# First block of a two-block transformer kernel: four pairs of weight parts, an own PSUM bank for the convolution, its layer norm later, both column halves of the projection at once

## The chip, the cores and the metric

One core of a Trainium2 chip runs the whole kernel. The metric is the device time of one execution in microseconds; 1314.99 us is the median of three runs of the kernel before (1314.49 to 1316.63).

## What is computed

Two transformer blocks over 256 tokens of width 1024, in float32. The first block, which the change touches, has three parts, each behind an RMS norm and added to the residual stream:

```python
proj = h @ w_in                      # q, k, v (512 columns each), 8 forget logits, 2 x 512 for the convolution
attn = rmsnorm(forgetting_attention(q, k, v, log_f), attn_out_g)           # 8 heads of 64, causal
conv = silu(layernorm(depthwise_conv31(a * sigmoid(gate)) + b_dw, ln_g, ln_b))
x = x + concatenate([attn, conv], -1) @ w_out
x = x + memory_cross_attention(h, rmsnorm(mem), w_mq, w_mkv, w_mo)         # 256 memory rows, 4 heads of 256
x = x + hierarchical_moe(h, ...)     # 32 experts; a token goes to 2 of the 8 experts of one group
```

The second block (a gated recurrence, a sparse attention and a feed-forward network) is as it was.

## The kernel before

**Matmuls in parts.** A large product is done with both operands split into a rounded part and a remainder. `wload` (line 164) has SP fetch a chunk of 4 x 128 weight rows by 512 columns (1 MB) into one of four `ring` buffers. `wsplit` (170) turns it into two half-chunks; for each, ACT rounds (`wh`, line 184) and DVE takes the remainder (`wl`, line 185) into a pair of the pool `hl`, which has three pairs. TensorE then does three matmuls for each 128 rows: high by high, high by low, low by high. In `dense_T` (216) the tokens are the moving operand (256 columns), so a half-chunk of four 128-column pieces is 24 matmuls of 256 columns; in `dense_nat` (197) the weights are the moving operand, and a half-chunk is 12 matmuls of 512 columns. A ring buffer comes free with its last `wl`, a pair of `hl` with its last matmul.

**The first block (`block1`, 390).** The squares of x are summed on ACT (`sq`), its rows are scaled by DVE and ACT (`ENG[0]`), transposed, and split into `xT`. The products with `w_in` follow: gates and values of the convolution with the forget logits, then q, k, v. The convolution of 31 taps takes two of its four channel groups on DVE, accumulated in the PSUM tile `ca` (452 to 460), and two on ACT and GpSimd: ACT multiplies a shifted slice into a buffer `zt` (three of them), GpSimd adds it to `zc` (466 to 471). Line 462 copies `ca` to `zc`. The attention (527 to 555) has for each pair of heads scores in the PSUM pool `ptr`, exponentials on ACT (324), transposes of the probabilities (540), copies to `PT` and products with the values into two PSUM tiles `po` of one bank each. Both `po` and `ca` are allocated from the pool `pat` of two buffers. After the attention come the keys and values of the memory (`mem_k`, `mem_v`: two chunks of 512 columns each), with the steps of the convolution's layer norm between them (`mu`, `va`, `vr`, 569 to 597), the norm and transposes of the attention (599 to 606), the projection `w_out` one column half after the other (620), the memory attention and its projection `w_mo`.

**Where the experts' weights go.** Line 607 closes the pool `be` of early tiles. What it held, and other buffers as they come free, makes up 24 slots of 1 MB (`more`, `mload`): 9 + 4 (`ring`) + 2 + 2 + 2 + 3 (`hl`) + 2. One group of four experts is 24 loads, and SP issues all expert loads of a group into these slots in a fixed order; each waits for the slot's last reader. The first five may be issued ahead of the last load of `w_mq`, the others behind it (`BEFORE`, 693).

**What sets the order.** The Tile scheduler orders each engine's instructions ahead of time by priority and by its own model of time. Priority is the order in the program; `high_priority(offset)` moves an instruction ahead, a negative offset (`LATER` = 300) back. On the chip each queue then runs in that order. Weight loads and splits are `AHEAD` = 1000 places early, the taps of the convolution 300 to 1200 places late.

Of the kernel before, what the change touches and what calls it, by code (L numbers as in the profile page):

```python
# [16 lines left out]
S = 256  # L17
# [10 lines left out]
PIECES = ((0, 512), (512, 512)), ((0, 512), (512, 256), (768, 256))  # L28
ENG = ("VA", "PP", "VA", "VA")
NRB, NR2, NRC, NRE, NRD = 9, 2, 2, 2, 2  # L30
NS4, NPM, NPT, NPA, NHP = 16, 3, 2, 1, 2
# [106 lines left out]
class B:  # L138
# [189 lines left out]
    def build(self, upto=99):  # L328
        tc, nc, A = self.tc, self.nc, self.A
        with ExitStack() as ctx:  # L330
# [3 lines left out]
            self.ring = E(tc.tile_pool(name="ring", bufs=4))  # L334
            self.hl = E(tc.tile_pool(name="hl", bufs=3))
            self.X = X = cp.tile([128, 2, D], F32, name="X")
# [53 lines left out]
    def block1(self):  # L390
        tc, nc, A = self.tc, self.nc, self.A
        V = nc.vector
        with tc.tile_pool(name="sm1", bufs=1) as self.sm, tc.tile_pool(name="b1", bufs=1) as b1, \
                tc.tile_pool(name="ptr", bufs=2, space=PSUM) as self.ptr, \
                tc.tile_pool(name="pat", bufs=2, space=PSUM) as self.pat:
            X = self.X
# [11 lines left out]
            with tc.high_priority(offset=100000):  # L408
                z0 = be.tile([128, S], F32, name="zt", bufs=3)
# [5 lines left out]
                self.busy(z0[:, :128], z0, WARM[4])  # L415
                for h, c in halves:
                    self.sq(X[:, h, c * 512:(c + 1) * 512], self.ss[:, h, c:c + 1])
                for h in range(2):
                    self.rfin(self.ss[:, h, :], self.rx[:, h:h + 1])
# [31 lines left out]

            ca = self.pat.tile([128, NCV, S], F32, name="po")
            wd, bd = self.vec("w_dw"), self.vec("b_dw")
            for i in range(4):
                zi, w = zc[:, i, :], lambda j: wd[:, i * 31 + j:i * 31 + j + 1]
                with tc.high_priority(offset=-LATER * (i + 1)):
                    if i < NCV:
                        V.tensor_scalar(ca[:, i, :], z[:, i, 0:S], w(0), bd[:, i:i + 1], op0=OP.mult, op1=OP.add)
                        for j in range(1, 31):
                            V.scalar_tensor_tensor(ca[:, i, :], z[:, i, j:j + S], w(j), ca[:, i, :], op0=OP.mult, op1=OP.add)  # L460
                        if i == NCV - 1:
                            nc.scalar.copy(zc[:, :NCV, :], ca)
# [63 lines left out]
            nmx = self.sm.tile([128, 2, 8], F32, name="nmx")  # L526
            po = [self.pat.tile([128, 8, 64], F32, name="po") for _ in range(2)]
            for h2 in range(0, 8, 2):
                P = be.tile([128, 2, 384], F32, name="P", bufs=2)
                for hf, kb, c0 in ((0, 128, 0), (1, 256, 128)):  # L530
# [4 lines left out]
                    self.exps(sc, P[:, :, c0:c0 + kb], kb, nmx[:, hf, h2:h2 + 2], sums[:, hf, h2:h2 + 2])  # L535
                PT = be.tile([128, 2, 384], F32, name="PT", bufs=2)
                for i in range(2):
                    pt = self.ptr.tile([128, 384], F32, name="tr")
                    for b in range(3):
                        nc.tensor.transpose(pt[:, b * 128:(b + 1) * 128], P[:, i, b * 128:(b + 1) * 128],  # L540
                                            self.cst("ident"))
                    if i % 2:
                        V.tensor_copy(PT[:, i, :], pt)
                    else:
                        nc.scalar.copy(PT[:, i, :], pt)
                    h = h2 + i
                    c = slice(h * 64, h * 64 + 64)
                    self.mm(po[0][:, h, :], PT[:, i, 0:128], v[:, 0, c], True, True)
                    self.mm(po[1][:, h, :], PT[:, i, 128:256], v[:, 0, c], True, False)
                    self.mm(po[1][:, h, :], PT[:, i, 256:384], v[:, 1, c], False, True)  # L550
            rc = self.sm.tile([128, 2, 8], F32, name="rc")
# [16 lines left out]
            mem_k(0)  # L568
            mu = self.pmm.tile([128, S], F32, name="mm")
            for i in range(4):  # L570
                self.mm(mu, self.cst("ones"), zc[:, i, :], i == 0, i == 3)
            xc = be.tile([128, 4, S], F32, name="xc")
            V.scalar_tensor_tensor(xc, mu[:, None, :].to_broadcast([128, 4, S]), -1.0 / 512, zc, op0=OP.mult, op1=OP.add)
            x2 = be.tile([128, 4, S], F32, name="zc")
            nc.scalar.activation(x2, xc, AF.Square)
            mem_k(1)
            va = self.pmm.tile([128, 2], F32, name="mm")
            for h in range(2):
                for i in range(4):
                    self.mm(va[:, h:h + 1], x2[:, i, h * 128:(h + 1) * 128], self.cst("ones")[:, 0:1], h + i == 0, i == 3)  # L580
            vs = self.sm.tile([128, 2], F32, name="vs")
            V.tensor_scalar(vs, va, 1.0 / 512, EPS, op0=OP.mult, op1=OP.add)
            nc.gpsimd.tensor_tensor(vs, vs, self.mhalf.to_broadcast([128, 2]), op=OP.pow)
            mem_v(0)
            vr = self.pmm.tile([128, S], F32, name="mm")
            for h in range(2):
                d = be.tile([128, 128], F32, name="dg", bufs=2)
                V.tensor_scalar(d, self.cst("ident"), vs[:, h:h + 1], None, op0=OP.mult)
                self.mm(vr[:, h * 128:(h + 1) * 128], self.cst("ones"), d, h == 0, True)
            cT = self.parts(b1x)  # L590
            cg, cb = self.vec("conv_ln_g"), self.vec("conv_ln_b")
            for i in range(4):
                V.scalar_tensor_tensor(xc[:, i, :], xc[:, i, :], cg[:, i:i + 1], vr, op0=OP.mult, op1=OP.mult)
                nc.scalar.activation(xc[:, i, :], xc[:, i, :], AF.Identity, bias=cb[:, i:i + 1])
            self.silu2(xc, xc, x2)
            nc.scalar.activation(cT[0](4, 4), xc, AF.Copy, scale=0.5)
            V.scalar_tensor_tensor(cT[1](4, 4), xc, 0.5, cT[0](4, 4).bitcast(F32), op0=OP.mult, op1=OP.subtract)
            mem_v(1)
            so = self.sm.tile([128, 2], F32, name="so")
# [4 lines left out]
            for h in range(2):  # L604
                self.scaled(o[:, h, :], o[:, h, :], so[:, h:h + 1], ENG[2])
            self.norm_T([o[:, 0, :], o[:, 1, :]], "attn_out_g", cT, 512)
            early.__exit__(None, None, None)
            self.slots, self.pools = [], []
            self.more(NRB)

            def resid(c):
# [25 lines left out]
            with tc.high_priority(offset=MAT):  # L637
                for h2 in range(0, 4, 2):
                    Pm = [None, None]
                    for hf in range(2):  # L640
                        sc = self.pat.tile([128, 2, S], F32, name="po")
                        for i in range(2):
# [12 lines left out]
                    for i in range(2):  # L655
# [6 lines left out]
                        V.tensor_copy(PT, pt)  # L662
                        po2 = self.pat.tile([128, 2, S], F32, name="po")
                        for d in range(2):
# [6 lines left out]
            self.more(NRE)  # L671
            self.slots += [self.hl] * 3
            pl = [self.pat.tile([128, 36], F32, name="po") for _ in range(2)]
            self.y = [[None, None], [None, None]]
# [1037 lines left out]
```

## Time and profile before

| | us |
|---|---|
| median of three runs | 1314.99 |
| the profiled execution | 1313.91 |
| its span, first to last instruction | 1311.9 |
| TensorE busy | 1197.4 (91%) |
| VectorE / ScalarE / GpSimd busy | 593.9 / 482.5 / 123.1 |
| mean granted TensorE clock | 0.967 of full speed |

Times in the rows are microseconds from the span's start. PE is TensorE's matmuls, PEld its weight loads, DVE VectorE, ACT ScalarE, POOL GpSimd, SP the queue that issues most transfers. "idle before <- X" is how long the engine had stood still and what ended it. Matmuls are pipelined, so their own durations overlap; the time of one is the step from its start to the next start. The granted clock is a share of full speed: 1.00 is 2.4 GHz, 0.50 is 1.2 GHz, and a figure between is a mean over a stretch.

### The profile page before, as it was taken

How to read it: one execution, taken by the hardware profiler on the slowest of the kernel's cores; microseconds unless marked ns; L12 is line 12 of the kernel's file. 1: busy time of each engine (PE TensorE's matmuls, PEld its weight loads, DVE VectorE, ACT ScalarE, POOL GpSimd, SP SyncE). 2: the span in 40 equal slices, each digit the busy share in tenths (PEclk: the TensorE clock that was granted, in tenths of full speed). 3: DMA queues.
4: the chain of work that ended last, by engine and by line, in shares of the span. 5: the costliest groups of instructions: out<-in, count | busy, mean ns of one | idle time of the engine just before them, and what ended most of it. 6: DMA issues, size and time to landing. Idle time of an engine off the chain costs nothing.

```text
span 1311.9 us, 17829 instructions
## 1 busy us (share of the span) xinstructions
PE 1197.4 (91%) x7122; PEld 877.0 (67%) x7122; DVE 593.9 (45%) x1031; ACT 482.5 (37%) x917; POOL 123.1 (9%) x171
## 2 busy tenths in 40 slices
PE   8897999989978878786958999999999999999997
PEld 7887888844432323141414898888888878989886
DVE  4875655510100000010003687666866667555665
ACT  6686644300000000000004543344666546544553
POOL 4875000000000000000001000014100000000000
PEclk9898999989989898898989999999999999999999
DMA  8431596869999999999999554543532346555551
GB/s 311 138 129 65 195 405 253 331 242 418 419 418 420 418 420 418 420 418 420 417 410 324 173 165 129 175 161 98 171 119 65 114 137 212 188 197 188 193 193 48
DMA packets 106360, 332.38 MB, mean 253 GB/s; under 512 B 6368, under 2 KB 20512, under 8 KB 85408
## 3 DMA queue, kind: packets, MB, share of 16 engines
q1 hardware_dynamic: 105712, 329.87, 66.7%
q10 hardware_dynamic: 560, 1.31, 0.3%
q8 instruction: 58, 0.95, 0.3%
q14 instruction: 30, 0.25, 0.1%
HBM read 330.11 MB, written 1.05 MB: 252 GB/s over the span
## 4 chain that ended last, share of the span: by engine, by line
PE 62%; DMA 29%; ACT 4%; DVE 2%; POOL 1%; issue 1%; SPq 0%; POOLq 0%; DVEq 0%; ACTq 0%
PE mm L195 40%; DMA w<-w_up_in 11%; DMA w<-w_gate_in 8%; PE z L195 7%; PE po L195 4%; DMA w<-w_down_in 4%; DMA wh<-w_down_in 4%; PE bg L195 3%; PE hp L195 2%; DMA wl<-w_down_in 2%; PE tr L195 1%; PE sp L195 1%; ACT wh L184 1%; POOL zc L471 1%; DMA w<-w_in_in 1%
## 5 line engine op out<-in xcount | busy, mean ns | idle before, releaser
L185 DVE TENSOR_TENSOR wl<-w,wh 128x1024 fp32r<-128x1024 f32 (+2 forms) x228 | 276.3, 1226 | 158.9 <-ACT wh L184 157.7
L184 ACT CAST wh<-w 128x1024 fp32r<-128x1024 f32 (+2 forms) x228 | 235.3, 1044 | 196.7 <-PE mm L195 155.0
L195 PE MATMUL bg<-w,xs 128*32 128x512 f32 x1024 | 177.4, 705 | 70.7 <-DMA w<-w_up_in 49.4
L195 PE MATMUL mm<-xTh,wl 128*128 128x256 f32 x688 | 193.8, 286 | 7.0 <-DVE wl L185 6.9
L195 PE MATMUL mm<-xTh,wh 128*128 128x256 f32 x688 | 188.7, 287 | 4.5 <-issue 2.0
L195 PE MATMUL mm<-xTl,wh 128*128 128x256 f32 x688 | 191.5, 284 | 0.1
L195 PEld LDWEIGHTS bg<-w,xs 128*32 128x32 f32 x1024 | 40.2, 125 | 200.1 <-issue 87.8
L195 PE MATMUL mm<-wl,xTh 128*128 128x512 f32 (+1 forms) x440 | 172.5, 395 | 0.3 <-DVE wl L185 0.3
L195 PE MATMUL mm<-wh,xTh 128*128 128x512 f32 (+1 forms) x440 | 167.6, 399 | 3.0 <-ACT xTh L251 1.0
L195 PE MATMUL mm<-wh,xTl 128*128 128x512 f32 (+1 forms) x440 | 169.9, 393 | 0.0
L195 PEld LDWEIGHTS mm<-xTh,wl 128*128 128x128 f32 x688 | 130.3, 190 | 10.3 <-DVE wl L185 9.7
L195 PEld LDWEIGHTS mm<-xTh,wh 128*128 128x128 f32 x688 | 127.5, 190 | 7.5 <-issue 2.6
L195 PEld LDWEIGHTS mm<-xTl,wh 128*128 128x128 f32 x688 | 129.9, 190 | 0.7 <-DVE xTl L253 0.3
L991 DVE SCALAR_TENSOR_TENSOR sg<-bg,rsl,sg 128x512 f32<-128x512 f32 x8 | 6.0, 751 | 250.5 <-PE bg L195 250.5
L195 PEld LDWEIGHTS mm<-wh,xTh 128*128 128x128 f32 x440 | 82.1, 188 | 20.3 <-ACT xTh L252 1.3
L195 PEld LDWEIGHTS mm<-wh,xTl 128*128 128x128 f32 x440 | 82.6, 188 | 17.8 <-issue 0.7
L195 PEld LDWEIGHTS mm<-wl,xTh 128*128 128x128 f32 x440 | 82.8, 188 | 17.3 <-DVE wl L185 1.0
L195 PE MATMUL bg<-w,ht 128*32 128x512 f32 x320 | 71.7, 597 | 1.3 <-ACT ht L999 0.7
L195 PEld LDWEIGHTS sp<-oh,X 128*128 128x128 f32 x256 | 61.2, 328 | 9.4 <-issue 9.2
L195 PE MATMUL sp<-oh,X 128*128 128x128 f32 x256 | 64.0, 401 | 0.0
L999 ACT COPY ht<-sp 128x512 f32<-128x512 f32 x8 | 4.7, 586 | 149.7 <-PE sp L997 149.7
L471 POOL TENSOR_TENSOR zc<-zc,zt 128x256 f32<-128x256 f32 x60 | 55.4, 924 | 14.0 <-ACT zt L468 9.6
(411 smaller groups left out, 1527.8 us busy)
## 6 DMA issues: line engine op xcount, KB each, us to landing
w<-w_up_in SPq DMA_DIRECT2D x80, 1024.0 KB, 19.9
w<-w_gate_in SPq DMA_DIRECT2D x64, 1024.0 KB, 16.2
w<-w_down_in SPq DMA_DIRECT2D x56, 1024.0 KB, 15.0
w<-w_in_in SPq DMA_DIRECT2D x41, 1024.0 KB, 5.3
wl<-w_down_in SPq DMA_DIRECT2D x24, 512.0 KB, 13.8
wh<-w_down_in SPq DMA_DIRECT2D x24, 512.0 KB, 16.2
w<-w_mkv_in SPq DMA_DIRECT2D x8, 1024.0 KB, 5.1
w<-w_out_in SPq DMA_DIRECT2D x8, 1024.0 KB, 5.0
```

What stands on the lines that cost most here:

```text
L184: self.nc.scalar.copy(hv, raw[:, j:j + g, :])
L185: self.nc.vector.tensor_tensor(lv, raw[:, j:j + g, :], hv.bitcast(F32), op=OP.subtract)
L195: return self.nc.tensor.matmul(out, lhsT, rhs, start=start, stop=stop, skip_group_check=True)
L471: nc.gpsimd.tensor_tensor(zi, zi, t, op=OP.add)
L991: V.scalar_tensor_tensor(sg, ps, rsl[q], sg, op0=OP.mult, op1=OP.mult)
L999: nc.scalar.copy(ht, tp)
```

## The change

Cut to its core; the lines that were moved unchanged are left out, and the text below says where they went.

```diff
-ENG = ("VA", "PP", "VA", "VA")
-NRB, NR2, NRC, NRE, NRD = 9, 2, 2, 2, 2
+ENG = ("VV", "PP", "VA", "VA")
+NRB, NR2, NRC, NRE, NRD = 9, 2, 2, 2, 1
...
-            self.hl = E(tc.tile_pool(name="hl", bufs=3))
+            self.hl = E(tc.tile_pool(name="hl", bufs=4))
...
-                tc.tile_pool(name="pat", bufs=2, space=PSUM) as self.pat:
+                tc.tile_pool(name="pat", bufs=1, space=PSUM) as self.pat:
...
                 for h, c in halves:
-                    self.sq(X[:, h, c * 512:(c + 1) * 512], self.ss[:, h, c:c + 1])
+                    x, a = X[:, h, c * 512:(c + 1) * 512], self.ss[:, h, c:c + 1]
+                    if h:
+                        V.tensor_tensor_reduce(j1, x, x, 1.0 / 1024, 0.0, OP.mult, OP.add, a)
+                    else:
+                        self.sq(x, a)
...
-            ca = self.pat.tile([128, NCV, S], F32, name="po")
+            ca = self.pat.tile([128, NCV, S], F32, name="po1")
...
-                        t = be.tile([128, S], F32, name="zt", bufs=3)
+                        t = be.tile([128, S], F32, name="zt", bufs=6)
...
-            self.setup()
+            with tc.high_priority(offset=-LATER):
+                self.setup()
...
-            po = [self.pat.tile([128, 8, 64], F32, name="po") for _ in range(2)]
...
+                if h2 % 4 == 0:
+                    po = self.pat.tile([128, 2, 4, 64], F32, name="po0")
...
-            V.reciprocal(rc, sums)
-            for hf in range(2):
-                V.tensor_tensor(o[:, hf, :].rearrange("p (h d) -> p h d", h=8), po[hf],
-                                rc[:, hf, :, None].to_broadcast([128, 8, 64]), op=OP.mult)
+                if h2 % 4:
+                    hs = slice(h2 - 2, h2 + 2)
+                    V.reciprocal(rc[:, :, hs], sums[:, :, hs])
+                    V.tensor_tensor(o.rearrange("p a (h d) -> p a h d", h=8)[:, :, hs], po,
+                                    rc[:, :, hs, None].to_broadcast([128, 2, 4, 64]), op=OP.mult)
...
-            for c in range(2):
-                self.dense_nat(cT, A["w_out"], D, c * 512, 512, resid(c))
+            ps = [[self.pmm.tile([128, 512], F32, name="mm") for _ in range(2)] for _ in range(2)]
+            for kg in (0, 4):
+                for c in range(2):
+                    wh, wl = self.wchunk(A["w_out"][kg * 128:(kg + 4) * 128, c * 512:(c + 1) * 512], 4, 512)
+                    for h in range(2):
+                        for k in range(4):
+                            a, b = (t(kg + k)[:, h * 128:(h + 1) * 128] for t in cT)
+                            self.mm(ps[c][h], a, wh[k], kg + k == 0, False)
+                            self.mm(ps[c][h], a, wl[k], False, False)
+                            self.mm(ps[c][h], b, wh[k], False, kg + k == 7)
+                    if kg:
+                        for h in range(2):
+                            resid(c)(h, ps[c][h])
...
-            self.slots += [self.hl] * 3
+            self.slots += [self.hl] * 4
```

The program's order after the attention was: mem_k(0), mean of the convolution, mem_k(1), variance, mem_v(0), its spread over the channels, the rest of the layer norm, mem_v(1), norm and transposes of the attention, projection. It becomes: mem_k(0), norm and transposes of the attention, mem_k(1), mean, mem_v(0), variance, mem_v(1), spread and rest of the layer norm, projection. The attention fills rows 0 to 511 of the projection's input (kg 0), the convolution rows 512 to 1023 (kg 4). The memory attention and the router use `po0` and `po1` in turn where they used the two buffers of `po`.

## Rows read from the trace of the kernel before

**Rows 1.** Stretches: length; busy PE, PEld, DVE, ACT, POOL; granted clock; DMA share; GB/s.
```profile
40.00:120.00 80.00, 67.43 (x429) 59.82 (x428) 63.57 (x101) 63.56 (x140) 63.60 (x65) 0.89 0.37 122
120.00:260.00 140.00, 137.83 (x824) 120.68 (x822) 78.48 (x146) 68.08 (x123) 4.49 (x6) 1.00 0.71 271
280.00:700.00 420.00, 339.04 (x1798) 130.13 (x1798) 28.47 (x53) 19.22 (x37) 0.00 (x0) 0.92 1.02 417
700.00:1312.00 612.00, 597.78 (x3694) 521.19 (x3692) 398.23 (x668) 306.57 (x571) 36.78 (x75) 1.00 0.47 156
```

**Rows 2.** The chain that ended last, behind the router: start, us, what.
```profile
278.29 0.22 SPq L871
...
279.08 16.89 DMA w<-w_gate_in
```

**Rows 3.** SP's queue in order of time, expert loads and loads around them.
```profile
157.36 2.78 SPq L871 DMA_DIRECT2D w<-w_gate_in  x5
161.40 17.20 SPq L167 DMA_DIRECT2D w<-w_mq_in  x4
...
252.61 0.48 SPq L871 DMA_DIRECT2D wh<-w_down_in  x1
274.63 5.93 SPq L871 DMA_DIRECT2D w<-w_gate_in  x8
```

**Rows 4.** What PE waited for, 20 to 120 us: us in total, times, longest.
```profile
PE mm L195 <- DVE wl L185: 5.4, 6, 1.8
PE tr L540 <- ACT P L324: 3.6, 3, 1.5
PE po L195 <- ACT zc L462: 2.7, 1, 2.7
```

**Rows 5.** PE in order of time: two plain steps, then the gap behind 105 us.
```profile
93.16 0.28 PE L195 MATMUL mm<-xTh,wl 128*128 128x256 f32 x1
93.28 0.28 PE L195 MATMUL mm<-xTl,wh 128*128 128x256 f32 x1
...
105.40 0.28 PE L195 MATMUL mm<-xTl,wh 128*128 128x256 f32 x1
...
113.78 2.61 PE L195 MATMUL po<-v,PT 128*128 128x64 f32 x11 [2.73 <-ACT zc L462]
...
119.36 0.47 PE L195 MATMUL mm<-xTh,wh 128*128 128x256 f32 x1
```

**Rows 6.** Stretches again, ten microseconds in the gap.
```profile
110.00:120.00 10.00, 7.12 (x29) 6.31 (x30) 3.32 (x6) 5.63 (x15) 6.53 (x9) 0.54 0.31 105
```

**Rows 7.** ACT in order of time: scaling of x, the convolution's copy, splits in the projection.
```profile
9.55 1.33 ACT L285 ACTIVATE mX<-X,rx 128x512 f32<-128x512 f32 x2
...
113.16 0.56 ACT L462 COPY zc<-po 128x512 f32<-128x512 f32 x1
...
167.45 1.05 ACT L184 CAST wh<-w 128x1024 fp32r<-128x1024 f32 x1 [1.75 <-PE mm L195]
170.24 1.05 ACT L184 CAST wh<-w 128x1024 fp32r<-128x1024 f32 x1 [1.74 <-PE mm L195]
```

**Rows 8.** Groups by line: DVE and POOL from 40 us, last row DVE 140 to 200.
```profile
L185 DVE TENSOR_TENSOR wl<-w,wh 128x1024 fp32r<-128x1024 f32 x18 | 23.2, 1290 | 7.9 <-ACT wh L184 7.8
L492 DVE TENSOR_SCALAR kz<-cc 8x1024 f32<-8x1024 f32 x2 | 4.6, 2282 | 0.0
L471 POOL TENSOR_TENSOR zc<-zc,zt 128x256 f32<-128x256 f32 x60 | 55.4, 924 | 14.0 <-ACT zt L468 9.6 <-DVE xTl L253 0.8
L185 DVE TENSOR_TENSOR wl<-w,wh 128x1024 fp32r<-128x1024 f32 x20 | 24.4, 1223 | 18.5 <-ACT wh L184 18.4
```

**Rows 9.** DVE in order of time: the attention's output, the layer norm's end.
```profile
132.05 1.28 DVE L554 TENSOR_TENSOR o<-po,rc 128x512 f32<-128x512 f32 x2
...
150.69 1.66 DVE L593 SCALAR_TENSOR_TENSOR xc<-xc,vc,mm 128x256 f32<-128x256 f32 x4 [0.64 <-PE mm L195]
156.91 1.23 DVE L597 SCALAR_TENSOR_TENSOR xTl<-xc,xTh 128x1024 fp32r<-128x1024 f32 x1
```

More of the change, by code (lines that the diff above doesn't have):

```diff
@@ L408, in block1 @@
             with tc.high_priority(offset=100000):
-                z0 = be.tile([128, S], F32, name="zt", bufs=3)
+                z0 = be.tile([128, S], F32, name="zt", bufs=6)
                 V.memset(z0, 0.0)
@@ L415, in block1 @@
                 self.busy(z0[:, :128], z0, WARM[4])
+                j1 = be.tile([128, 512], F32, name="junk1")
                 for h, c in halves:
-                    self.sq(X[:, h, c * 512:(c + 1) * 512], self.ss[:, h, c:c + 1])
+                    x, a = X[:, h, c * 512:(c + 1) * 512], self.ss[:, h, c:c + 1]
[3 more added lines that the diff above has]
+                        self.sq(x, a)
                 for h in range(2):
@@ L526, in block1 @@
             nmx = self.sm.tile([128, 2, 8], F32, name="nmx")
-            po = [self.pat.tile([128, 8, 64], F32, name="po") for _ in range(2)]
+            rc = self.sm.tile([128, 2, 8], F32, name="rc")
             for h2 in range(0, 8, 2):
@@ L547, in block1 @@
                     c = slice(h * 64, h * 64 + 64)
[L548 to L551, printed above, removed]
-            V.reciprocal(rc, sums)
-            for hf in range(2):
-                V.tensor_tensor(o[:, hf, :].rearrange("p (h d) -> p h d", h=8), po[hf],
-                                rc[:, hf, :, None].to_broadcast([128, 8, 64]), op=OP.mult)
+                    self.mm(po[:, 0, h % 4, :], PT[:, i, 0:128], v[:, 0, c], True, True)
+                    self.mm(po[:, 1, h % 4, :], PT[:, i, 128:256], v[:, 0, c], True, False)
+                    self.mm(po[:, 1, h % 4, :], PT[:, i, 256:384], v[:, 1, c], False, True)
+                if h2 % 4:
[3 more added lines that the diff above has]
+                                    rc[:, :, hs, None].to_broadcast([128, 2, 4, 64]), op=OP.mult)
             self.tap("o", o)
@@ L568, in block1 @@
             mem_k(0)
[L569 to L589, printed above, removed]
-            cT = self.parts(b1x)
[L591 to L598, printed above, removed]
+            cT = self.parts(b1x)
             so = self.sm.tile([128, 2], F32, name="so")
@@ L606, in block1 @@
             self.norm_T([o[:, 0, :], o[:, 1, :]], "attn_out_g", cT, 512)
+            mem_k(1)
+            mu = self.pmm.tile([128, S], F32, name="mm")
+            for i in range(4):
+                self.mm(mu, self.cst("ones"), zc[:, i, :], i == 0, i == 3)
+            xc = be.tile([128, 4, S], F32, name="xc")
+            V.scalar_tensor_tensor(xc, mu[:, None, :].to_broadcast([128, 4, S]), -1.0 / 512, zc, op0=OP.mult, op1=OP.add)
+            x2 = be.tile([128, 4, S], F32, name="zc")
+            nc.scalar.activation(x2, xc, AF.Square)
+            mem_v(0)
+            va = self.pmm.tile([128, 2], F32, name="mm")
+            for h in range(2):
+                for i in range(4):
+                    self.mm(va[:, h:h + 1], x2[:, i, h * 128:(h + 1) * 128], self.cst("ones")[:, 0:1], h + i == 0, i == 3)
+            vs = self.sm.tile([128, 2], F32, name="vs")
+            V.tensor_scalar(vs, va, 1.0 / 512, EPS, op0=OP.mult, op1=OP.add)
+            nc.gpsimd.tensor_tensor(vs, vs, self.mhalf.to_broadcast([128, 2]), op=OP.pow)
+            mem_v(1)
+            vr = self.pmm.tile([128, S], F32, name="mm")
+            for h in range(2):
+                d = be.tile([128, 128], F32, name="dg", bufs=2)
+                V.tensor_scalar(d, self.cst("ident"), vs[:, h:h + 1], None, op0=OP.mult)
+                self.mm(vr[:, h * 128:(h + 1) * 128], self.cst("ones"), d, h == 0, True)
+            cg, cb = self.vec("conv_ln_g"), self.vec("conv_ln_b")
+            for i in range(4):
+                V.scalar_tensor_tensor(xc[:, i, :], xc[:, i, :], cg[:, i:i + 1], vr, op0=OP.mult, op1=OP.mult)
+                nc.scalar.activation(xc[:, i, :], xc[:, i, :], AF.Identity, bias=cb[:, i:i + 1])
+            self.silu2(xc, xc, x2)
+            nc.scalar.activation(cT[0](4, 4), xc, AF.Copy, scale=0.5)
+            V.scalar_tensor_tensor(cT[1](4, 4), xc, 0.5, cT[0](4, 4).bitcast(F32), op0=OP.mult, op1=OP.subtract)
             early.__exit__(None, None, None)
@@ L619, in resid @@
                 return f
-            for c in range(2):
-                self.dense_nat(cT, A["w_out"], D, c * 512, 512, resid(c))
+            ps = [[self.pmm.tile([128, 512], F32, name="mm") for _ in range(2)] for _ in range(2)]
+            for kg in (0, 4):
+                for c in range(2):
+                    wh, wl = self.wchunk(A["w_out"][kg * 128:(kg + 4) * 128, c * 512:(c + 1) * 512], 4, 512)
+                    for h in range(2):
+                        for k in range(4):
[4 more added lines that the diff above has]
+                    if kg:
+                        for h in range(2):
+                            resid(c)(h, ps[c][h])
             self.tap("x1", X)
@@ L640, in block1 @@
                     for hf in range(2):
-                        sc = self.pat.tile([128, 2, S], F32, name="po")
+                        sc = self.pat.tile([128, 2, S], F32, name=f"po{hf}")
                         for i in range(2):
@@ L662, in block1 @@
                         V.tensor_copy(PT, pt)
-                        po2 = self.pat.tile([128, 2, S], F32, name="po")
+                        po2 = self.pat.tile([128, 2, S], F32, name=f"po{i}")
                         for d in range(2):
@@ L671, in block1 @@
             self.more(NRE)
-            self.slots += [self.hl] * 3
-            pl = [self.pat.tile([128, 36], F32, name="po") for _ in range(2)]
+            self.slots += [self.hl] * 4
+            pl = [self.pat.tile([128, 36], F32, name=f"po{h}") for h in range(2)]
             self.y = [[None, None], [None, None]]
```

## Prediction

> **What bounds the kernel now.** I read the stretches first, to see which engine is full in which part. From 700 us on TensorE is busy 597.8 of 612 us [rows 1]: the second block is matmul-bound and the change hardly reaches it. From 280 to 700 us the transfers run at 417 GB/s with a share of 1.02, and TensorE waits for them: the experts' stage is bound by its transfers. When that stage ends depends on when its stream restarts. I read this in the chain of waits behind the router: SP issues at 278.29, released by an expert matmul, and from there transfer follows transfer [rows 2]. SP's own queue says the same: the last prefetch goes out at 252.61, the next expert loads from 274.63, each when a slot has been read [rows 3]. So the router and all of the first block ahead of it are on the path, and a microsecond saved there should arrive whole at the end.
>
> Inside the first block, 120 to 260 us has TensorE busy 137.8 of 140 at full clock: nothing to gain. From 40 to 120 it is busy 67.4 of 80 at a mean granted clock of 0.89 [rows 1], that is 67.4 x 0.89 = 60 us of full-speed work. Of the 20 us lost, 12.6 are idle and 7.4 went to stretches at 1.2 GHz. The waits name the causes: 5.4 us for remainders of weights (`wl`), 3.6 for probabilities, 2.7 for the copy of the convolution out of PSUM [rows 4]; these are 11.7 of the 12.6.
>
> **The change part by part.** *(a) An own bank for the convolution, six `zt`.* The second `po` of the attention needs the buffer that `ca` holds until line 462, and that copy stands on ACT at 113.16, behind taps. TensorE's plain matmuls stop at 105.40 and go on at 119.36; in between it waits for probabilities and then, at 113.78, for the copy [rows 5, 7]. A plain step is 0.12 us, so the gap is 13.8 us. Ten of them are at a mean clock of 0.54 with 7.12 us busy, 3.8 us of full-speed work [rows 6]; the 4.6 us ahead of 110 hold a few transposes, which I put at under 1 us. So about 9 us of this gap is loss. The wait for the copy goes altogether, the eleven products behind it spread out, and the slow clock, which followed the pause, should go with it. The waits for probabilities stay in part, since ACT is busy 63.6 of 80 us here [rows 1]. I take 7.5 of the 9; the bounds are 2.7 (the one wait alone) and 9.
>
> *(b) A fourth pair of weight parts.* The splitting can run one half-chunk further ahead: 24 matmuls of 0.12 us [rows 5], 2.9 us of TensorE's time, more than the longest wait of 1.8 [rows 4]. What (a) leaves of the 20 us, 11, is these waits and the slow clock after them. But a deeper buffer does not make the splitters faster: a `wl` comes late because DVE is taken, by two writes of `kz` of 2.28 us each, for example [rows 8]. I take a third, 3.5, within 0 and 11.
>
> DVE, ACT and POOL are each busy 63.6 us in this stretch, and that work does not shrink. If all of it had to be done before 120 us, (a) and (b) together could give at most 80 - 63.6 = 16.4. Some of the convolution may run over, as DVE has 61 us free between 120 and 260 [rows 1] and the mean is now taken two steps later.
>
> *(c) The start.* Scaling x leaves ACT, where 1.33 us stood between the first weights and the first `xTh` [rows 7]. DVE gets these two scalings and two sums of squares, which the trace does not show on DVE. I bound (c) by 0 and 1.3 and take 0.7, the middle, because DVE also has the first `wl` to make.
>
> *(d) New waits.* Heads 4 to 7 now need the one bank of heads 0 to 3 read first: half of 1.28 us for the product [rows 9] and a reciprocal, about 1 us. TensorE has weights of `mem_k` to work on meanwhile; behind it in its queue, if it does stand, are those matmuls. Cost 0 to 1, taken 0.3. In the projection the residual of column half 0 comes late: both halves finish within the last half. A half-chunk of 12 matmuls takes 2.79 us there (167.45 to 170.24) [rows 7], so half 0 is complete 5.6 us ahead of the end and not 11.2. The addition, transposes and splits of its first rows of `xT` have to fit in that. Cost 0 to 2, taken 0.5. The two exponentials of `setup`, 300 places later, may come behind the logarithm of the forget gates and cost ACT a table load; 0 to 1.3 in its queue, in front of taps and splits; taken 0.4.
>
> *(e) The layer norm later.* From its last scaling to its last part it takes 150.69 to 158.14, 7.45 us [rows 9], on DVE and ACT. Now it follows `mem_v(1)`, and the projection needs it for kg 4 alone. Ahead of that stand 48 matmuls, four half-chunks, 11.2 us. The cover is 3.7 us longer than the chain: cost nothing; without the cover, up to 7.45 us. The early pool closes behind this chain, and with it start the first expert loads, at 157.36 in the kernel before [rows 3]. After the change the chain starts about 10 us earlier relative to the clock (as the whole block does) but one step of `mem_v`, also about 11 us, later in the order. So these loads start at about the same time.
>
> *(f) Slots and the second block.* 9 + 4 + 2 + 2 + 2 + 4 + 1 = 24 slots, as before, so the first stream holds as much. In the second block 14 us of TensorE idle time [rows 1] is all that a fourth pair could touch, and a new order could lose as much as it gains there: 0, within -2 and +2.
>
> The sum: 7.5 + 3.5 + 0.7 - 0.3 - 0.5 - 0.4 = 10.5 us. The profiled execution took 1313.91 (span 1311.9 and 2.0 around it), so 1303.4; the median of the runs is 1.1 higher, which gives 1304.5 us.
>
> **The rivals.** *Splitters stay the bound.* The planner fills ACT and DVE by its own times; with six `zt` ACT takes even more taps ahead of splits and exponentials, and TensorE meets other late `wl`. For it: three engines at 79% busy in a queue order fixed beforehand. Against it: nothing in the stretch runs longer than before. Then only the wait for the copy and some clock come back: 3.5 us, 1311.5.
>
> *DVE and POOL hold each other up.* A `wl` took 1290 ns on average beside POOL's additions (18 of them) and 1223 without (20) [rows 8], so 1.2 us in all is paid today. POOL stood idle 14 us between its additions [rows 8]; six `zt` close these gaps, and if each of 18 splits then had to sit out one whole addition of 0.92, DVE would be busy 18 x 0.92 - 1.2 = 15.4 us more, 79 us in the stretch: no more than 1 us of (a) and (b) left, and 1314.5 with it. *The Trainium skill ("SBUF — State Buffer", section "SBUF: two separate sides") says that a VectorE instruction with two SBUF inputs and a GpSimd instruction that reads SBUF exclude each other for a whole instruction.* The trace bears out a small part of it so far, 67 of 924 ns.
>
> *The layer norm comes onto the path (slower).* If the scheduler puts its steps behind the projection's splits on DVE and ACT, or if an accumulator of the projection has to wait for the bank of `vr` (four of the four banks are now held at once), TensorE stands between kg 0 and kg 4 or ahead of kg 0. Price: 7.45 us [rows 9], and behind such a pause the clock falls, as at 110 to 120, where 0.54 over 10 us cost 4.6 [rows 6]: 12 us, 1.6 more than the gain, 1316. With the variance steps in it as well it may be 1320. It decides from 10.5 us of new pauses on. For it: TensorE has nothing else to do there. Against it: the cover of 3.7 us.
>
> *The saving does not arrive.* SP's queue is in order; the first expert loads wait for the early pool, `w_mq` follows 4 us behind [rows 3]. If the pool closes some 10 us later than I reckon, `w_mq` or the last prefetch is late for TensorE by about as much as was saved: 1314. Against it: transfers are busy 0.71 of 120 to 260 [rows 1], so 40 us of the stream are unused.
>
> **How the numbers follow.** Forecast (gain 5 to 16): 0.60. Gain over 16, with the convolution spilling and (b) whole: 0.05, about 1297. Splitters: 0.15. Ports: 0.03. Layer norm on the path: 0.11. Not arriving: 0.06. The likeliest case alone spans 1299 to 1310. The range has to take in the splitters and the two cases at no change, with the low end from the cap of 16.4: 1298 to 1315. About 2.6 us, 0.2%, can be told from no change. Faster by that: 0.60 + 0.05 + 0.11 of the splitters = 0.76. Same: 0.04 of the splitters, 0.03, 0.06 = 0.13, of which 0.01 goes to slower. Slower: 0.11 + 0.01 = 0.12, same 0.12.
>
> **What would show it.** In the profile after: no wait of `po` for line 462, plain matmuls between the values of the heads, and a clock near 1.00 from 40 to 120 (a); the waits for `wl` at 2 to 3 us (b); a first matmul 0.5 to 1 us earlier (c); no idle time of TensorE between the two kg of the projection, and first expert loads at 155 to 160 (e); SP's restart at about 264 instead of 274.63, then 417 GB/s up to the second block. The prediction is wrong if the stretch from 40 to 120 shortens and the restart does not come earlier, or if the pauses come back at the projection.

## The result, and the profile after

The changed kernel takes 1325.00 us (median of five runs, 1324.42 to 1330.78) against 1314.88 for the kernel before on the same chip (five runs, 1313.48 to 1316.63): ratio 1.0084, interval 1.0071 to 1.0098. The forecast was 1304.5. It is slower by 10.1 us, outside the range, and by a way that no rival describes. The span of the profiled execution is 1322.7 us against 1311.9.

The same four stretches as in [rows 1], of the kernel after:

```profile
40.00:120.00 80.00, 68.93 (x481) 64.00 (x480) 62.97 (x99) 64.27 (x136) 67.68 (x64) 0.91 0.40 135
120.00:260.00 140.00, 132.80 (x764) 115.64 (x762) 77.59 (x147) 66.12 (x128) 3.62 (x6) 0.98 0.69 261
280.00:700.00 420.00, 337.32 (x1800) 129.89 (x1798) 28.39 (x53) 18.64 (x35) 0.00 (x0) 0.92 1.02 417
700.00:1312.00 612.00, 598.19 (x3669) 521.23 (x3664) 395.28 (x660) 306.26 (x566) 36.99 (x74) 0.99 0.47 156
```

From 40 to 120 us TensorE is busy 1.5 us longer, at a mean clock of 0.91 for 0.89; from 120 to 260, where it had been full, it now stands for 7.2 of 140 us. Two places must be looked at, the first block and the second, and two landmarks cut the span: SP's restart of the expert loads, and the end of the last expert matmul. SP's queue after, to compare with the restart at 274.63 [rows 3], then PE around the last expert matmul, before and after:

```profile
274.90 5.88 SPq L890 DMA_DIRECT2D w<-w_gate_in  x7
```

```profile
704.15 1.06 PE L195 MATMUL bg<-w,ht 128*32 128x512 f32 x8 [0.58 <-DMA w<-w_down_in]
```

```profile
704.78 1.07 PE L195 MATMUL bg<-w,ht 128*32 128x512 f32 x8 [0.57 <-DMA w<-w_down_in]
...
713.24 0.53 PE L195 MATMUL mm<-wh,xTh 128*128 128x512 f32 x1 [2.88 <-ACT sg L239]
```

The restart is 0.3 us later, not 10.5 earlier: the first block has gained nothing. The last expert matmul ends at 705.85 instead of 705.21. From there to the end of the span it takes 616.9 us instead of 606.7: of the 10.8 us by which the span grew, 10.2 are in the second block, whose code is the same.

**First block.** What TensorE waited for from 20 to 120 us, after (compare [rows 4]), and then from 120 to 260:

```profile
PE mm L195 <- ACT xTh L252: 5.5, 3, 3.7
PE tr L548 <- ACT P L324: 2.7, 1, 2.7
...
PE mm L195 <- DVE wl L185: 0.8, 1, 0.8
```

```profile
PE tr L272 <- DVE o L288: 5.1, 1, 5.1
```

The wait of `po` for the convolution's copy is gone and that for `wl` has fallen from 5.4 us to 0.8, further than the 2 to 3 that were forecast. In their place stand parts of the memory's normalised rows (`xTh`) and, at 155 to 160 us, the scaled output of the attention: no matmul was left to run beside the attention's tail. The tiles say why. Transposes (L272 of `mX`, the memory's norm among them) and scores, each with its duration and its first and last start; before, then after:

```profile
L272 PE MATMUL tr<-cs,mX x32: 270/273/327, 9.0 to 49.3; 128*128 128x128 f32 x32
...
L195 PE MATMUL tr<-kz,qz x32: 270/353/435, 75.4 to 122.9; 128*128 128x128 f32 x16, 128*128 128x256 f32 x16
```

```profile
L272 PE MATMUL tr<-cs,mX x32: 271/273/445, 9.0 to 89.0; 128*128 128x128 f32 x32
...
L195 PE MATMUL tr<-kz,qz x32: 271/352/436, 93.4 to 140.1; 128*128 128x128 f32 x16, 128*128 128x256 f32 x16
```

The last transpose of the memory's norm moves from 49.3 to 89.0 us, the first score from 75.4 to 93.4. Plain matmuls went ahead: the copies of `v` leave PSUM 6 to 7 us earlier. The block did the same work in another order, and the part with the long serial tail came last.

**Second block.** The same thing happens at the product with `w_ple`, which needs the small tile `pn` transposed and split. PE and ACT before (two fences), then after:

```profile
1087.10 0.60 PE L1239 MATMUL tr<-cs,pn 128*128 128x128 f32 x4
...
1089.85 0.40 PE L195 MATMUL mm<-wh,pTh 128*128 128x512 f32 x1
```

```profile
1087.77 0.58 ACT L251 CAST pTh<-tr 128x512 fp32r<-128x512 f32 x1
```

```profile
1092.85 0.60 PE L1258 MATMUL tr<-cs,pn 128*128 128x128 f32 x4
1096.21 0.79 PE L195 MATMUL mm<-wh,pTh 128*128 128x512 f32 x1 [2.77 <-ACT pTh L251]
```

```profile
1093.69 1.98 ACT L184 CAST wh<-w 128x1024 fp32r<-128x1024 f32 x2
1095.57 0.59 ACT L251 CAST pTh<-tr 128x512 fp32r<-128x512 f32 x1
```

Before, the transposes stood among the matmuls of `w_out_2`; the split was done at 1088.35 and had 1.3 us to spare, as its first weight load starts at 1089.62. After, they stand behind all of them, the split stands behind two `wh` of 0.99 us, and TensorE waits 2.77 us and then runs at a lower clock (0.77 from 1096.21 to 1103). Behind the product it waits once more, 2.88 us for the next split where the kernel before waited 2.04, and again the clock is lower: 0.55 from 1109.2 to 1113, against 1.00.

### The profile page after: what moved, and what is told of

The parts are those of the page before. It is cut to its first block, busy times and chain, and to the rows that moved or that the text cites. A ratio compares the mean times of both kernels' runs of the same rounds, so it can differ in the third digit from the quotient of the medians.

```text
span 1322.7 us, 17844 instructions
## 1 busy us (share of the span) xinstructions
PE 1197.9 (91%) x7122; PEld 880.7 (67%) x7122; DVE 596.7 (45%) x1038; ACT 481.3 (36%) x911; POOL 128.8 (10%) x171
## 4 chain that ended last, share of the span: by engine, by line
PE 48%; DMA 27%; DVE 1%; ACT 1%; issue 0%; SPq 0%; POOL 0%; DVEq 0%; POOLq 0%; ACTq 0%
PE mm L195 29%; DMA w<-w_up_in 9%; DMA w<-w_gate_in 8%; PE z L195 7%; DMA w<-w_down_in 5%; DMA wh<-w_down_in 3%; PE po L195 3%; PE hp L195 3%; PE bg L195 3%; PE sp L195 1%; DMA w<-w_in_in 1%; PE tr L195 1%; DMA wl<-w_down_in 1%; PE hp L1568 1%; PE tr L272 0%
## 5 line engine op out<-in xcount | busy, mean ns | idle before, releaser
L195 PE MATMUL mm<-xTh,wh 128*128 128x256 f32 x688 | 195.9, 287 | 9.4 <-ACT xTh L252 6.5
L195 PE MATMUL mm<-xTl,wh 128*128 128x256 f32 x688 | 194.3, 287 | 1.7 <-DVE xTl L253 1.7
L195 PE MATMUL mm<-wh,xTh 128*128 128x512 f32 (+1 forms) x440 | 173.5, 401 | 6.1 <-ACT sg L239 2.9
L195 PEld LDWEIGHTS mm<-xTh,wh 128*128 128x128 f32 x688 | 131.6, 192 | 12.2 <-ACT xTh L252 8.6
L195 PEld LDWEIGHTS sp<-oh,X 128*128 128x128 f32 x256 | 61.2, 328 | 10.2 <-issue 10.1
L476 POOL TENSOR_TENSOR zc<-zc,zt 128x256 f32<-128x256 f32 x60 | 58.2, 972 | 4.3
## 6 DMA issues: line engine op xcount, KB each, us to landing
w<-w_down_in SPq DMA_DIRECT2D x48, 1024.0 KB, 13.8
wl<-w_down_in SPq DMA_DIRECT2D x32, 512.0 KB, 13.8
```

The costliest lines, as they stand in the source:

```text
L195: return self.nc.tensor.matmul(out, lhsT, rhs, start=start, stop=stop, skip_group_check=True)
```

## The experiments

Sixteen kernels; median, the kernel before on the same chip, ratio with interval, the restart, and the second block (end of the last expert matmul to the end of the span) of the profiled execution. Before: 274.63 and 606.7. Restart and second block come from one execution of each kernel. The executions of one kernel spread by 2 to 9 us, and the profiled one lay up to 4.3 us above its median (order_four_memnorm) and 3.1 below (bank_alone, the shortest of its ten), so for a difference of a few microseconds the medians count. The ratios are not the quotients of the medians in the table; the two differ by up to 0.0015.

| run | us | before | ratio | restart | 2nd block |
|---|---|---|---|---|---|
| pairs_alone | 1321.01 | 1315.13 | 1.0043 [1.0030, 1.0057] | 273.29 | 616.1 |
| three_pairs | 1310.58 | 1315.13 | 0.9962 [0.9946, 0.9977] | 272.12 | 606.5 |
| four_then_three | 1317.29 | 1315.13 | 1.0001 [0.9987, 1.0015] | 278.59 | 606.8 |
| bank_alone | 1313.71 | 1315.13 | 0.9991 [0.9982, 1.0001] | 272.07 | 606.3 |
| ple_early | 1318.06 | 1315.37 | 1.0025 [1.0006, 1.0043] | 275.70 | 609.8 |
| ple_memnorm_early | 1309.98 | 1315.37 | 0.9956 [0.9942, 0.9970] | 265.12 | 609.8 |
| order_alone | 1308.64 | 1315.37 | 0.9941 [0.9923, 0.9960] | 270.10 | 606.1 |
| bank_start_three | 1310.20 | 1315.37 | 0.9962 [0.9947, 0.9977] | 270.92 | 606.6 |
| ple_late_three | 1319.72 | 1315.30 | 1.0038 [1.0025, 1.0052] | 276.59 | 611.1 |
| four_then_three_memnorm | 1301.57 | 1315.30 | 0.9898 [0.9873, 0.9923] | 262.47 | 606.2 |
| order_four_memnorm | 1308.63 | 1315.30 | 0.9947 [0.9929, 0.9965] | 271.25 | 606.2 |
| order_start | 1306.37 | 1315.30 | 0.9927 [0.9907, 0.9946] | 267.89 | 606.2 |
| transition_hold | 1310.37 | 1315.56 | 0.9958 [0.9944, 0.9972] | 265.65 | 610.0 |
| mem_k_ahead | 1310.64 | 1315.56 | 0.9963 [0.9950, 0.9976] | 273.41 | 606.3 |
| order_old_projection | 1307.54 | 1315.56 | 0.9941 [0.9918, 0.9964] | 267.06 | 607.8 |
| best_old_projection | 1303.71 | 1314.29 | 0.9928 [0.9905, 0.9952] | 263.06 | 605.8 |

**Is it the fourth pair?** Alone on the kernel before, and taken out of the changed one:

```diff
+NRB, NR2, NRC, NRE, NRD = 9, 2, 2, 2, 1
+            self.hl = E(tc.tile_pool(name="hl", bufs=4))
+            self.slots += [self.hl] * 4
```

> The kernel before with four pairs of weight parts instead of three (and the one expert slot that this costs) and nothing else. Theory A (the fourth pair lets weight splits, which have precedence, pass small steps that TensorE needs, and the second block loses by it): the second block is about 11 us longer than before, as in the changed kernel, and the first gains 2 to 8 us; total 1316 to 1324 us. Rival B (the second block's loss follows from the new order of the first block or from the shorter setup, not from the pairs): second block within 2 us of before, total 1306 to 1314 us.

> The changed kernel with three pairs of weight parts as before, all else as changed. Theory A: the second block is within 2 us of the kernel before, the first block keeps the own bank of the convolution and ends 3 to 8 us earlier; total 1307 to 1313 us. Rival B: the second block stays 11 us longer, total 1320 to 1326 us.

And four pairs in the first block only (`hl` has three, every fourth half-chunk goes to a pool `hlx` of one until the second block begins):

```diff
+            hl = self.hlx if self.hlx and self.nsp % 4 == 3 else self.hl
+            self.nsp += 1
```

> The changed kernel with four pairs in the first block and three from the second block on (the fourth half-chunk in turn goes to a pool of its own, which the second block does not use). Theory A: the first block as in the changed kernel (restart of the expert loads at 275 us), the second block as before: 1312 to 1316 us. Rival B: the second block stays 8 to 11 us longer, total 1322 to 1326 us.

In all three the second block follows the number of pairs, 616 with four and 606 to 607 with three, whatever the first block did: theory A holds for the second block, and rival B falls. In the first block A erred. four_then_three restarts at 278.59, not 275 (in the longest of its ten executions), and its median is 1.3 us above the expected range; three_pairs gains 2.5 us there and not 3 to 8.

**What does the fourth pair do to the second block?** The transposes of `pn` and their split go early with four pairs, and late with three (two edits in one cut, each named in a comment):

```diff
+                with tc.high_priority(offset=400):        # ple_early
+                with tc.issue_after(self.lastmm.ins):     # ple_late_three: last matmul of w_out_2
                     for i in range(2):
...
                             nc.tensor.transpose(ps[:, i, h * 128:(h + 1) * 128], pn[:, h, ...
```

> The changed kernel (four pairs) with one edit in the second block: the transposes of pn and their split (pTh, pTl), which the product with w_ple needs, take precedence by 400 places. Theory A2 (with the fourth pair the planner packs the matmuls of w_out_2 together and the transposes of pn come behind all of them, so no matmul is left to cover the split and the norm behind it): the transposes stand among w_out_2 again, product and pause of 10.9 us shrink to 6 us, and the second block is 6 to 9 us shorter than in the changed kernel (608 to 611): 1316 to 1319 us. Rival D (the fourth pair costs mainly at the start of the second block, where wh and wl stand ahead of sq and xTh): at most 3 us come back, 1322 to 1325 us.

> The kernel before, three pairs, with one edit: the transposes of pn may be issued only behind the last matmul of w_out_2, where the fourth pair had put them. Theory A2 (their lateness, not the splits themselves, costs most of the second block's loss): the second block grows by 4 to 9 us, 611 to 616, total 1319 to 1324 us. Rival G (with three pairs the split of pT is not passed by wh and wl, so it costs only the split itself): under 2 us, 1315 to 1317 us.

PE in ple_late_three, where the three pairs are untouched:

```profile
1091.24 0.60 PE L1240 MATMUL tr<-cs,pn 128*128 128x128 f32 x4
1093.66 0.50 PE L195 MATMUL mm<-wh,pTh 128*128 128x512 f32 x1 [1.82 <-ACT pTh L251]
```

Early, 7.1 of the 10.2 us come back, and rival D falls; late, 4.4 us are lost without any fourth pair, the pause of 1.82 us and the lower clock behind it among them, and rival G falls. So lateness alone is about 4.4, and lateness in the order of four pairs about 7; that the splits ahead of `pTh` make the difference is likely but has no run of its own. Of the remaining 3.1 us (609.8 against 606.7) I thought that they were the splits ahead of `sq` and `xTh` at 710 us:

```diff
-            self.holdq = [[]] + [[last]] * 2
+            self.holdq = [[]] + [[last]] * 3
```

> The changed kernel (four pairs throughout) with three edits: pn's and the memory norm's transposes 400 places ahead, as in the run with both, and at the start of the second block the fourth half-chunk's split is held behind the same instruction as the second and third. Theory A2: the 3.3 us by which the second block was still longer there (609.8 against 606.5) were this passing at the start; now 606 to 607.5, total 1304 to 1308 us. Rival H (the fourth pair costs in the middle of the second block as well): 609 to 610, 1308 to 1312 us.

The run has ScalarE's instructions in the same order as ple_memnorm_early, so it says nothing of the hold. But in both TensorE's wait for `sg` there is 0.8 us as in the kernel before (2.88 in the changed one), and the second block is still 610: the loss is not at that place alone, and rival H, or a part of it, stands. The trace of ple_memnorm_early shows where it is: at the product with `w_ple` again. Counted from the last expert matmul, the product starts 1.3 us later than in the kernel before. Behind it TensorE waits 0.7 us longer for the next split, and then does 21 matmuls in 4.1 us at a mean clock of 0.59, where the kernel before did 35 at 1.00, worth 1.6 us. That is 3.6 us, of which 3.1 are left at the end. The first matmul behind the product, before and in ple_memnorm_early:

```profile
1099.38 0.35 PE L195 MATMUL mm<-xTh,wh 128*128 128x256 f32 x1 [2.04 <-issue]
```

```profile
1095.70 0.39 PE L196 MATMUL mm<-xTh,wh 128*128 128x256 f32 x1 [2.77 <-DVE xTl L254]
```

**What lost the gain of the first block?** The memory norm's transposes early as well:

```diff
+            with tc.high_priority(offset=400):
                 mT = self.norm_T([mX[:, 0, :], mX[:, 1, :]], "mem_norm_g", self.parts(b1y))
```

> As the run before, and in the first block the transposes of the memory's norm (mX to mT) also take precedence by 400 places. Theory A2 in the first block (these transposes, and the scores behind them in the same PSUM pool, come too late for the tail of the attention to be covered): they end before 60 us instead of 89, the scores begin before 80 instead of 93, TensorE no longer waits 5.1 us for the scaled o, and the restart of the expert loads comes at 268 to 271: 1310 to 1314 us. Rival E (the attention is late because ACT and DVE are full, not because of the transposes): scores still begin after 88 us and the restart stays at 274 to 276: 1316 to 1319 us.

```profile
L273 PE MATMUL tr<-cs,mX x32: 272/273/421, 8.7 to 52.0; 128*128 128x128 f32 x32
...
L196 PE MATMUL tr<-kz,qz x32: 270/352/435, 70.2 to 131.1; 128*128 128x128 f32 x16, 128*128 128x256 f32 x16
```

```profile
265.12 6.02 SPq L892 DMA_DIRECT2D w<-w_gate_in  x8
```

The transposes end at 52, the scores begin at 70, the wait for `o` is gone and the restart comes at 265.12, 10.6 us earlier than in ple_early; the prediction's own figure was 264. Rival E falls. Of the 10.6 us 3.5 are lost in the experts' stage of this execution, where the clock is at 1.2 GHz (0.50) for some of the last steps (`mm<-od,pt` x4 takes 3.78 us there and 1.98 in four_then_three_memnorm). The median gains 8.1 us on ple_early. With three pairs in the second block:

> The changed kernel with four pairs in the first block and three in the second, and the transposes of the memory's norm 400 places ahead. Theory A2: restart at 264 to 268 as in the run with both precedences, second block 606 to 607: 1302 to 1307 us. If the early restart is taken back at the end of the experts' stage by a slow clock there (3.8 us in the run with both precedences): 1306 to 1309 us.

```profile
40.00:120.00 80.00, 74.45 (x527) 69.37 (x526) 67.40 (x104) 67.73 (x147) 67.94 (x66) 0.98 0.42 139
120.00:260.00 140.00, 137.04 (x778) 117.15 (x781) 75.24 (x160) 62.57 (x118) 4.53 (x6) 0.99 0.70 261
```

This is the best version, 1301.57 us, faster than both kernels: 74.5 us busy from 40 to 120 at 0.98, against 67.4 at 0.89 [rows 1], and the stretch behind it loses only 3 us.

**What is each other part worth?** bank_alone has the own bank, heads in fours and six `zt`; order_alone the new order with the joint projection; bank_start_three all but the order; order_start no bank; order_four_memnorm the best version without bank, `zt` and start.

> The kernel before with the own PSUM bank of the convolution, the attention's output in one bank for four heads at a time, and six buffers for the taps; pairs, order and start as before. The prediction's step (a): restart of the expert loads 5 to 8 us earlier, at 267 to 270, second block unchanged: 1307 to 1310 us. Rival C (the early gain is lost later in the first block, because the attention's tail stands where no matmul covers it): restart within 2 us of 274.63, 1313 to 1317 us.

> The kernel before with only the new order (attention's norm after mem_k(0), layer norm later, both halves of the projection at once); three pairs, two buffers of po as before. If the order costs nothing in itself (the prediction's step (e) and half of (d)): restart within 1 us of 274.63, 1313.5 to 1316 us. Rival F (the order eats the gain of the first block): a pause of 3 to 6 us ahead of the projection and the restart at 277 to 281, 1317 to 1321 us.

> The changed kernel with three pairs and with the order of the kernel before: the own bank of the convolution, six buffers for the taps and the new start remain. Against the run with three pairs (residual finished at 178.49, restart at 272.12) it tells what the order does. If the order is neutral: restart at 271 to 273, 1309 to 1312 us. If the order gave the earlier residual: residual at 181 to 183, restart at 272 all the same. If the order costs: restart at 268 to 270, 1306 to 1308 us.

> The kernel before with the new order and the new start (x scaled by VectorE, two sums of squares on it, setup later), three pairs, po and ca as before. The prediction's step (c) says that the start gives 0.7 us (0 to 1.3): restart at 268.8 to 270.1, 1307 to 1309 us. Rival (the start costs, as VectorE also makes the first wl): restart later than 270.5, above 1309 us.

> The kernel before with the new order, four pairs in the first block and three in the second, and the transposes of the memory's norm 400 places ahead; po, ca, zt and the start as before. If the fourth pair is worth something in the first block once these transposes come early: restart 1 to 5 us ahead of the new order alone (270.10), 1303 to 1308 us. If it is worth nothing without the own bank: restart at 270 to 273, 1308 to 1311 us.

By the restart the bank gives 2.6 us, half of the lowest expectation; but this is the shortest of its executions, the median gains 1.4 us, within rival C's 1313 to 1317, and the interval of its ratio includes 1. What follows is by the restart, with the median behind it. The order, which was to be neutral, gives 4.5 us (6.7); the start 1.2 (3.5) on top of the bank and 2.2 (2.3) on top of the order. They don't add up: with three pairs order and start give 6.7 (8.9), order, start and bank 2.5 (4.6). With four pairs and early transposes the bank, `zt` and start are worth 8.8 us (7.1); without them the fourth pair is worth nothing, 1308.63 us against 1308.64 in order_alone. The stretch from 100 to 120 us, columns as in [rows 1], in the kernel before, bank_alone and order_alone:

```profile
100.00:120.00 20.00, 13.69 (x78) 12.01 (x77) 11.82 (x21) 13.81 (x35) 15.31 (x19) 0.74 0.31 105
```

```profile
100.00:120.00 20.00, 15.75 (x96) 13.88 (x95) 12.62 (x21) 10.65 (x28) 10.66 (x11) 0.83 0.28 102
```

```profile
100.00:120.00 20.00, 18.23 (x140) 17.21 (x140) 15.66 (x25) 16.69 (x39) 17.07 (x18) 1.00 0.39 130
```

The order fills the gap that step (a) was to close, with `po` and `ca` in one pool as before. One line of it, and the order without the joint projection:

```diff
             mem_k(0)
+            mem_k(1)
             mu = self.pmm.tile([128, S], F32, name="mm")
...
-            mem_k(1)
```

> The kernel before with one line moved: mem_k(1) ahead of the convolution's mean instead of behind it. Theory J (the gap of TensorE behind 105 us stood because mem_k(1) was queued behind the mean, which waits for the convolution; the new order gained by that): the copies of the second mem_k come 8 to 11 us earlier than 135.5, the restart 2.5 to 4.5 us earlier than 274.63, 1308 to 1312 us. Rival K (the new order gained at the projection, by taking both column halves at once): restart within 1 us of 274.63, 1314 to 1316 us.

> The kernel before with the new order but the projection one column half after the other, as before. Theory J: restart as with the new order (270.10) or up to 1 us off it, 1307 to 1310 us; without the joint projection the layer norm has 5.6 us less cover, so a pause of up to 2 us may stand ahead of kg 4 and the restart come at 271 to 272. Rival K: restart at 273 to 276, 1313 to 1316 us.

> The changed kernel with four pairs in the first block and three in the second, the transposes of the memory's norm 400 places ahead (as in the run of 1301.6 us), and the projection one column half after the other, as before the change. With three pairs and the new order, the joint projection moved the restart from 267.06 to 270.10, 3.0 us. If that holds here: restart at 259 to 261 instead of 262.47, 1298 to 1300 us. If the joint projection only cost there because of where the clock fell: restart within 1 us of 262.47, 1300.5 to 1303 us.

In mem_k_ahead the gap is filled (18.13 us at 1.00 from 100 to 120, the last `mem_k` copy at 129.2 instead of 139.0), so `mem_k(1)` had stood behind the convolution's mean. But the restart gains 1.2 us only: from 120 to 150 TensorE works 28.56 us at 0.89 instead of 30.00 at 1.00, behind a wait of 1.4 for the attention. The median gains 4.9 us, which is in theory J's range (1308 to 1312); the execution profiled, of 1312.19 us, was the second longest of ten. So theory J explains the gap, and between 1.2 and 4.9 us of the order's gain. Rival K falls: without the joint projection the order keeps its gain and is 3.0 us better at the restart (1.1 in the median), with four pairs 0.6 us worse (263.06 for 262.47; 2.1 in the median). What the joint projection costs is open; so is which other step of the order gives the rest.

## Why the prediction was wrong

**The step that failed is (f)** ("In the second block 14 us of TensorE idle time [rows 1] is all that a fourth pair could touch, and a new order could lose as much as it gains there: 0, within -2 and +2."). The runs show +9.5 (pairs_alone) and +10.2 us. That sentence bounded what more cover can gain and took the same figure for what a new order can lose. What the traces show is that with four pairs the plain matmuls close up and the small work of the next phase comes behind them. Why the planner does so is my reading and not shown: that it had put this work where it reckoned with a wait for a split. On the chip TensorE waited only 0.3 us between 1060 and 1090 us in the kernel before.

**(b)** was right in its size where it was looked for: the wait for `wl` fell by 4.6 us. But the sum put 10.5 us at the restart, and there the changed kernel measured 0.3 the other way: this is the other half of the miss of 20.5 us. The step that failed there is the same, on the first block: no term stood for what a fourth pair does to the order. Alone it moved the restart by 1.3 us, with the last transpose of the memory's norm at 86.7 us, as in the changed kernel (89.0) and not as with three pairs (49.3 before, 54.9 in three_pairs); with these transposes early the restart came 10.6 us earlier.

**(a)** was sized by the whole gap of 13.8 us [rows 5, 6], 7.5; the waiting row gives 2.7, and 2.6 came at the restart, 1.4 in the median. The gap had two causes in a row, and the second, `mem_k(1)` behind the mean, does not appear in a list of waits, since an instruction that is not yet at the head of its queue waits for nothing. Even the whole gap was not worth the 9 us of the prediction: mem_k_ahead filled it for 1.2 us at the restart, 4.9 in the median. Two readings were loose besides: [rows 4] begin at 20 us, and 0.7 of the 5.4 us for `wl` lie ahead of 40; and a clock of 0.54 over ten microseconds with 7.12 of work costs 3.3 us, not 4.6 [rows 6].

**(c)** 0.7 forecast, 1.2 and 2.2 measured at the restart, 3.5 and 2.3 in the medians. **(d)** 0.5 forecast as the cost of the late residual; 3.0 or -0.6 at the restart, 1.1 or -2.1 in the medians, open. Its other two terms no run tells apart. **(e)** The layer norm did stay off the path in the changed kernel, as said: its last part ends at 163.8, and TensorE has no pause between the two kg. But the order as a whole was not neutral; it is the largest single gain with three pairs.

The rivals: "Splitters stay the bound" fell with the wait for `wl`. The ports cost VectorE little (a `wl` took 1326 ns on average from 40 to 120 us with POOL's idle time down from 14.0 to 4.3 us, against 1290 [rows 8]: 0.7 us over 20 of them), because it is mostly POOL that waits. The prediction looked at VectorE alone, and its reading "67 of 924 ns" is wrong. Three `wl` of the kernel before, then two of POOL's additions:

```profile
40.60 1.22 DVE L185 TENSOR_TENSOR wl<-w,wh 128x1024 fp32r<-128x1024 f32 x1
42.12 1.22 DVE L185 TENSOR_TENSOR wl<-w,wh 128x1024 fp32r<-128x1024 f32 x1
59.10 1.70 DVE L185 TENSOR_TENSOR wl<-w,wh 128x1024 fp32r<-128x1024 f32 x1
```

```profile
42.13 1.81 POOL L471 TENSOR_TENSOR zc<-zc,zt 128x256 f32<-128x256 f32 x1
...
74.28 0.74 POOL L471 TENSOR_TENSOR zc<-zc,zt 128x256 f32<-128x256 f32 x1 [0.34 <-ACT zt L468]
```

The addition at 74.28 has no `wl` beside it and takes 0.74 us, where the mean of 60 is 924 ns [rows 8]; the one that starts with the `wl` of 42.12 takes 1.81 and ends 0.6 us behind it. The `wl` of 59.10 starts 0.1 us into an addition and takes 1.70 instead of 1.22. In the changed kernel four `wl` are of this kind (1.65 to 1.72 us). *The Trainium skill ("SBUF — State Buffer", section "SBUF: two separate sides") has such a pair exclude each other for a whole instruction, whichever starts first; the trace agrees.* "Layer norm onto the path" had the sign and the place where pauses came back, ahead of the projection, but by the attention's norm, the other of the two that the change moved.

What the prediction named as its disproof came about in both halves: 40 to 120 got better and the restart did not, and a pause stood ahead of the projection.

## What to carry to other kernels

Deeper buffers don't only remove waits: a planner may order everything anew, in every stage that shares the buffer, as it did here in both blocks. Where a wait is removed, list the small steps that ran among the matmuls there (transposes, splits, norms of the next phase), and give them precedence in the same edit; confine the buffer to the stage that needs it. And read a gap from the queue, not only from the wait that ended it: ask what the next plain matmul is, and what stands ahead of it in program order.

## What the runs showed of the hardware

A pause of the same length costs more or less by the clock behind it. At the end of the experts' stage, where the code is the same, the kernel before and bank_start_three have the same two pauses; behind the second the same four matmuls take 1.98 us at a granted clock of 1.00 and 3.78 at 0.50 (before, then bank_start_three):

```profile
694.67 1.05 PE L195 MATMUL bg<-wl,ht 128*32 128x512 f32 x4 [1.47 <-DMA wl<-w_down_in]
696.47 1.98 PE L195 MATMUL mm<-od,pt 128*128 128x512 f32 x4 [0.74 <-ACT od L1022]
```

```profile
690.94 1.76 PE L195 MATMUL bg<-wl,ht 128*32 128x512 f32 x4 [1.45 <-DMA wl<-w_down_in]
693.44 3.78 PE L195 MATMUL mm<-od,pt 128*128 128x512 f32 x4 [0.73 <-ACT od L1030]
```

This is worth 2 to 4 us of the total: the stage from restart to last expert matmul lasted 430.6 to 431.1 us in the profiled executions of thirteen of the eighteen kernels, before and after among them, and 432.6 to 434.4 in five. In each of these five the execution is above its kernel's median, so it may belong to the execution and not to the kernel. Differences of 2 or 3 us between two orders of the first block should not be read as the worth of an edit.
